# A hybrid S5 / RG-LRU / GLA block on one core: decay logarithms in a new layout, value weights by single blocks, decays behind the chain, and a new order at the turn to the up projection

## The chip, the core and the metric

The kernel runs on one core of a Trainium2 chip. The metric is the time of one execution on the device in microseconds (us), the median of several runs. A core has a matrix engine (TensorE, PE in the profile), a vector engine (VectorE, DVE), a scalar engine (ScalarE, ACT), GpSimd (POOL), and SyncE (SP), which here only issues DMA transfers. Each engine works through its own instructions in order and waits on semaphores for the others. PE's results go to PSUM, from where DVE or ACT fetch them.

## The reference

One layer of a backbone over 1024 latent tokens, with 256 context tokens ahead of them, 1024 channels, in float32. All inputs are given to the kernel.

```python
u  = rms_norm(x) * (1 + scale) + shift        # and the same for the context
zl = split(u @ w_in);  zc = split(uc @ w_in)  # 5408 columns: S5, LRU x2, q, k, v, g, z, gates
s5  = S5 scan both ways over zl[0], then a gated linear unit
lru = RG-LRU both ways over a short convolution of zl[1], times gelu(zl[2])
gla = chunked gated linear attention, 4 heads, both ways, over q, k, v with the decay
      log_a = log_sigmoid(z[:, 16 d : 16 d + 16] @ w2[d] + b2[d]) / 16
y  = (g0 * (s5 @ w0) + g1 * (lru @ w1) + g2 * (gla @ w2)) @ w_out
h  = x + gate * y
u  = rms_norm(h) * (1 + scale) + shift
h  = h + gate * ((silu(conv3(u @ up)[gate half]) * conv3(u @ up)[value half]) @ down)
out = rms_norm(h)
```

The recurrent mixers scan the context first and start the latent scan from its final state. The 32 columns z, sixteen for each direction, give 512 decay logarithms for each token: four blocks of 128 rows, two per direction.

## The kernel before

Every matrix product is done in three passes of rounded halves: weights and activations are split into a high part (line 214, a cast on ACT) and a rest (line 215, a subtraction on POOL or DVE), called wh and wl for weights, uh and ul for the normed latent tokens, uch and ucl for the context. The output of a product of 512 tokens lies in a PSUM tile "ma" or "mb", of 256 context tokens in one of them; smaller things lie in four tiles "sm".

PE's instructions stand in the order in which the program is written (pe_order, line 444). The projections are a generator, proj_stream, whose parts the mixers interleave with their own products: at each point F(name) a mixer draws as many microseconds of projection work as the table FILL says. A second generator, background, makes the decay logarithms; one piece of it, a matmul on line 653 and its followers, comes after every BG-th step of the value projection. The projections stop at markers ("lru", "pc", "kv", "g") until the mixer allows them on. For the other engines the scheduler decides what stands where, except in a stretch at the start (start_order) and one at the turn to the up projection (norm_order, lines 1770 to 1891, and turn_order behind it), where the program's order holds.

The work before and around the change, in order of time:

- The LRU's scans, up to about 249 us: ACT and DVE work on blocks of 128 channels and 1280 tokens (lines 953 to 990), beside q, k and context projections on PE.
- z_steps makes z. It loads wz, splits it into one of three wh buffers (lines 687 and 688), and multiplies (lines 691 to 702). z for the context lies in lsw[3], for the latents in lsw[2], all in partitions 0 to 63.
- decay_logs makes one piece of the logarithms: a matmul (line 653), Abs, Relu and Exp on ACT (658, 660, 661), then a polynomial in which ACT squares into a buffer "tmp" (665) and DVE multiplies it on (666), three times; POOL subtracts and a DMA takes the result away. There are three buffers "tmp", and the result r lies in one of them from line 660 until the DMA has read it. Eight pieces of 512 latent tokens come first, then four of 256 context tokens.
- v_steps makes the value projection of ten blocks of 128 tokens. For each half of the value columns it takes two weights at once (take(2)), each a wh and a wl, and goes over groups of four blocks with both; its results go out by line 733.
- S5, from about 339 us: its prepared state (lines 1148 to 1174), then the first of its products (1166, 1187, 1215), DVE's sums (1219 to 1222) and scans.
- GLA, from about 520 us: for each head, decays() makes the running sums (scans on lines 1287 and 1288, then 1291 to 1300) and states() runs an 18-step chain of the state (line 1362) and copies it out (1365, 1366). The next head's decays() stands in the program behind the present head's states and its first scores. Beside it PE makes projections (528 to 532), which ACT fetches (795, 606).
- The turn, 880 to 980 us: the output projection (284 to 286) leaves h, whose squares are added up (1729, 1730), summed over channels on PE (279) and spread again (273). The up projection's products are combinations of four token quarters (Strassen's and Winograd's way): product operands T1 to T4 and B11 to B22, weight combinations (1629), and results in PSUM banks bka to bkd (lines 839 to 841), read by lines 1641 to 1672. p1, p3 and p4 are such products; z57 copies C (1666), adds D (1667) and z (1668). Four subtractions of one h block from another stand on POOL (1752).

Of the kernel before, what the change touches and what calls it, by code (L numbers as in the profile page):

```python
# [82 lines left out]
BG = 4  # L83
# [26 lines left out]
def tile_kernel(tc, I, out, dbg=None):  # L110
# [567 lines left out]
    zw = []  # L678

    def z_steps():  # L680
# [7 lines left out]
        V.tensor_tensor(zz[:, :, 32:64], wz3, f32(zz[:, :, 0:32]), OP.subtract)  # L688
        p = one()
# [4 lines left out]
        zc = lsw[3][0:64, 0:256]  # L694
        S.copy(zc, p[0:64, 0:256])
# [12 lines left out]
        zw.append((zs + [zc], w2))  # L708

    def v_steps(blocks):  # L710
        for hv in range(2):
            ws = take(2)
            for b0 in range(0, len(blocks), 4):
                bs = blocks[b0:b0 + 4]
                p = two()
                for i, b, k in [(i, b, 4 * kh + k) for kh in range(2) for i, b in enumerate(bs) for k in range(4)]:
                        o = p[i // 2][:, i % 2 * 256:(i % 2 + 1) * 256]
                        h, l = ws[k // 4]
                        sl = slice((k % 4) * 256, (k % 4 + 1) * 256)
                        if b < 2:  # L720
                            ah, al = uch[:, k, b * 128:(b + 1) * 128], ucl[:, k, b * 128:(b + 1) * 128]
                        else:
                            j, bb = divmod(b - 2, 4)
                            ah, al = uh[j][:, k, bb * 128:(bb + 1) * 128], ul[j][:, k, bb * 128:(bb + 1) * 128]
                        last = k == KT - 1 and i % 2 == 1
                        PE.matmul(o, ah, h[:, sl], start=(k == 0 and i % 2 == 0), stop=False, skip_group_check=True)
# [4 lines left out]
                for i0 in range(0, len(bs), 2):  # L731
                    t = pt()
                    S.copy(t, p[i0 // 2])
                    S.dma_start(vsp[bs[i0] * 128:(bs[i0] + 2) * 128, hv * 256:(hv + 1) * 256]
                                .rearrange("(a t) v -> t a v", a=2), t.rearrange("p (a v) -> p a v", a=2))
# [7 lines left out]
    def proj_stream():  # L743
# [13 lines left out]
        yield from marker("lru")  # L757
        for b in range(2):
# [519 lines left out]
    class Head:  # L1278
# [59 lines left out]
        def states(self):  # L1338
# [22 lines left out]
            for step in range(1, 19):  # L1361
                V.scalar_tensor_tensor(Sd[:, step], Sd[:, step - 1], self.dec[:, step:step + 1], Sd[:, step],
                                       OP.mult, OP.add)
# [115 lines left out]
    for h in range(4):  # L1479
# [6 lines left out]
        head.scores(0)  # L1486
        if nxt:
            nxt.decays()
# [120 lines left out]
    class Pair:  # L1609
# [53 lines left out]

        def z57(self):
            w, z = self.gv[1][:, tl[0]], self.gv[1][:, tl[1]]
            S.copy(w, self.C)
# [44 lines left out]
    for j in range(2):  # L1711
        sl = tl[j]
        acc = pt()
        for m in range(8):
# [16 lines left out]
            if j == 1 and m == 3:  # L1731
                for i in range(2):
# [41 lines left out]
    for m in (6, 7):  # L1774
        SY.dma_start(hsp[m][:, tl[1]], hT[m][:, tl[1]])
    q[1].sums((5,))
# [4 lines left out]
    q[1].p1()  # L1781
    rq = rstd_cols(st, 4, small[:, 12:16])
    q[1].sums((6, 7))
# [3 lines left out]
    bcast(pr, rq, 4)  # L1787
    for i in range(2):
        product(q[i].A, q[i].w[2], B21, False)
# [85 lines left out]
    q[0].load(3, 4)  # L1875
    nxt.open("b")
# [12 lines left out]
    q[1].z6()  # L1889
    q[1].z57()  # L1890
# [8 lines left out]
    for i in range(2, HID):  # L1899
# [12 lines left out]
        product(pair.D, pair.w[7], T3, True)  # L1912
        pair.z57()
# [395 lines left out]
```

## Time and profile before

| | us |
|---|---|
| median of 3 runs (lowest, highest) | 1599.78 (1599.44, 1605.92) |
| the profiled execution | 1601.49 |
| its span | 1599.7 |
| PE busy in the span | 1521.8 (95%) |
| DVE busy | 1092.8 (68%) |
| ACT busy | 770.1 (48%) |
| POOL busy | 461.3 (29%) |

The profiled execution lasted 1.79 us more than its span, and 1.71 us more than the median. PE's idle time is what bounds the kernel from below: 78 us. The granted clock of PE has two levels, 1.2 and 2.4 GHz; a mean of 0.66 in a stretch of 5 us says that about two thirds of it were at the lower level.

### The profile page before, as it was taken

How to read it: one execution, taken by the hardware profiler on the slowest of the kernel's cores; microseconds unless marked ns; L12 is line 12 of the kernel's file. 1: busy time of each engine (PE TensorE's matmuls, PEld its weight loads, DVE VectorE, ACT ScalarE, POOL GpSimd, SP SyncE). 2: the span in 40 equal slices, each digit the busy share in tenths (PEclk: the TensorE clock that was granted, in tenths of full speed). 3: DMA queues.
4: the chain of work that ended last, by engine and by line, in shares of the span. 5: the costliest groups of instructions: out<-in, count | busy, mean ns of one | idle time of the engine just before them, and what ended most of it. 6: DMA issues, size and time to landing. Idle time of an engine off the chain costs nothing. (4 is left out here: it accounts for less than half of the span.)

```text
span 1599.7 us, 21566 instructions
## 1 busy us (share of the span) xinstructions
PE 1521.8 (95%) x8144; PEld 1254.7 (78%) x8144; DVE 1092.8 (68%) x1620; ACT 770.1 (48%) x1221; POOL 461.3 (29%) x291
## 2 busy tenths in 40 slices
PE   5999999799998999999999988999999999999997
PEld 4888867677886788788888767788888888878887
DVE  4533469879876624533461689888888888899962
ACT  4423766665543643443233455444444444444661
POOL 3313333431122323222236534333333333000032
PEclk9999999899999999999999999999999999999999
DMA  9763633221224244231474321222222222974203
GB/s 346 242 224 93 208 109 110 93 90 58 64 61 144 70 139 130 77 86 60 144 246 159 130 88 40 92 80 79 80 91 81 80 80 100 370 248 157 93 27 106
DMA packets 93785, 198.91 MB, mean 124 GB/s; under 512 B 13489, under 2 KB 34865, under 8 KB 93553
## 3 DMA queue, kind: packets, MB, share of 16 engines
q1 hardware_dynamic: 81968, 181.62, 33.9%
q10 hardware_dynamic: 11712, 15.91, 2.9%
q8 instruction: 64, 1.05, 0.3%
q14 instruction: 41, 0.33, 0.1%
HBM read 158.98 MB, written 38.52 MB: 123 GB/s over the span
## 5 line engine op out<-in xcount | busy, mean ns | idle before, releaser
L215 POOL TENSOR_TENSOR wl<-wr,wh 128x1024 fp32r<-128x1024 f32 (+2 forms) x87 | 183.4, 2109 | 455.7 <-ACT wh L214 428.5
L214 ACT CAST wh<-wr 128x1024 fp32r<-128x1024 f32 (+2 forms) x87 | 77.3, 891 | 139.6 <-issue 41.9
L215 POOL TENSOR_TENSOR wp<-tmp,wp 128x512 fp32r<-128x512 f32 x44 | 74.1, 1701 | 220.4 <-ACT wp L214 203.4
L528 PE MATMUL ma<-uh,wh 128*128 128x512 f32 x272 | 118.0, 434 | 4.5 <-ACT pt L795 4.5
L528 PE MATMUL mb<-uh,wh 128*128 128x512 f32 x272 | 107.2, 394 | 0.0
L530 PE MATMUL ma<-ul,wh 128*128 128x512 f32 x272 | 107.0, 393 | 0.0
L530 PE MATMUL mb<-ul,wh 128*128 128x512 f32 x272 | 106.9, 393 | 0.0
L532 PE MATMUL mb<-uh,wl 128*128 128x512 f32 x272 | 106.7, 392 | 0.0
L532 PE MATMUL ma<-uh,wl 128*128 128x512 f32 x272 | 106.4, 391 | 0.0
L214 ACT CAST wp<-tmp 128x512 fp32r<-128x512 f32 x78 | 46.5, 619 | 93.0 <-DVE tmp L1629 92.9
L1693 DVE SCALAR_TENSOR_TENSOR ca<-gv,vec,ca 128x1023 f32<-128x1023 f32 (+2 forms) x66 | 61.4, 954 | 23.7 <-ACT ca L1685 23.6
L214 ACT CAST wp<-hd 128x512 fp32r<-128x512 f32 x88 | 52.8, 618 | 49.1 <-PE bkd L1998 25.9
L214 ACT CAST wp<-wr 128x512 fp32r<-128x512 f32 x97 | 58.2, 620 | 36.4 <-DMA wr<-in_wdn_dram 17.4
L1696 DVE SCALAR_TENSOR_TENSOR ca<-gv,vec,ca 128x1023 f32<-128x1023 f32 (+2 forms) x66 | 70.6, 1093 | 0.1
L528 PEld LDWEIGHTS ma<-uh,wh 128*128 128x128 f32 x272 | 51.8, 190 | 20.7 <-issue 6.5
L2178 POOL TENSOR_TENSOR acc<-acc,tmp 128x256 f32<-128x256 f32 (+1 forms) x9 | 9.0, 1002 | 182.8 <-ACT tmp L2175 182.7
L215 DVE TENSOR_TENSOR wp<-hd,wp 128x512 fp32r<-128x512 f32 x88 | 60.7, 708 | 1.3 <-ACT wp L214 1.1
L530 PEld LDWEIGHTS ma<-ul,wh 128*128 128x128 f32 x272 | 51.6, 190 | 11.5
L532 PEld LDWEIGHTS ma<-uh,wl 128*128 128x128 f32 x272 | 51.4, 189 | 11.5
L532 PEld LDWEIGHTS mb<-uh,wl 128*128 128x128 f32 x272 | 51.3, 189 | 11.4
L530 PEld LDWEIGHTS mb<-ul,wh 128*128 128x128 f32 x272 | 51.3, 189 | 11.3
L528 PEld LDWEIGHTS mb<-uh,wh 128*128 128x128 f32 x272 | 52.0, 191 | 9.5 <-issue 1.4
(628 smaller groups left out, 4661.9 us busy)
## 6 DMA issues: line engine op xcount, KB each, us to landing
wa<-in_ada_dram SPq DMA_DIRECT2D x96, 256.0 KB
wr<-in_wup_dram SPq DMA_DIRECT2D x46, 512.0 KB
wr<-in_win_dram SPq DMA_DIRECT2D x40, 512.0 KB
wr<-in_wdn_dram SPq DMA_DIRECT2D x22, 512.0 KB
hd<-hid SPq DMA_DIRECT2D x22, 512.0 KB
hid<-ca SPq DMA_DIRECT2D x21, 512.0 KB
wr<-in_wout_dram SPq DMA_DIRECT2D x16, 512.0 KB
tmp<-in_wdn_dram SPq DMA_DIRECT2D x22, 256.0 KB
```

The source lines that it names most:

```text
L214: S.copy(h, src)
L215: lo.tensor_tensor(l, src, f32(h), OP.subtract)
L528: PE.matmul(p[j], h[:, kk], uh[j][:, k], start=f, stop=False)
L530: PE.matmul(p[j], h[:, kk], ul[j][:, k], start=False, stop=False)
L532: PE.matmul(p[j], l[:, kk], uh[j][:, k], start=False, stop=e)
L1693: V.scalar_tensor_tensor(a[:, t0_ + 1:t0_ + 1 + n1], x[:, o:o + n1], fw[0], a[:, t0_ + 1:t0_ + 1 + n1], OP.mult, OP.add)
L1696: V.scalar_tensor_tensor(a[:, t0_ + c - 1:t0_ + n - 1], x[:, o + c:o + n], fw[2], a[:, t0_ + c - 1:t0_ + n - 1], OP.mult, OP.add)
L2178: G.tensor_tensor(acc, acc, sq, OP.add)
```

## The change

Six edits. First, the z weights are split in a function of their own, z_prep, called at the marker "lru", into a buffer tmp instead of a wh; w2 is loaded twice, into partitions 0 to 63 and 64 to 127, and the two latent halves of z lie in these partition halves. Second, r lies in lsw[3] (two halves in turn) and no longer in a tmp; the context's z lies in a tmp. The four context pieces come first, and a piece comes after every sixth step instead of every fourth. Third, v_steps takes one weight at a time and goes over all blocks with it, with up to four PSUM tiles. Fourth, the next head's decays are issued after the last step of the present head's chain. Fifth, the four subtractions of h blocks go from POOL to DVE. Sixth, in the turn the products p1 and B21 stand elsewhere, and the copy of C is a step of its own, c57, ahead of the next product.

```diff
-BG = 4
+BG = 6
...
-            r = tmp()[:, :n]
+            r = lsw[3][:, par * 512:par * 512 + n]
...
-        zs, w2 = zw[0]
+        zs, zc, w2 = zw[0]
+        yield from decay_logs(0, 256, zc, w2[0])
         for j in range(2):
-            yield from decay_logs(C + j * 512, 512, zs[j], w2)
-        yield from decay_logs(0, 256, zs[2], w2)
+            yield from decay_logs(C + j * 512, 512, zs[j], w2[j])
...
+    def z_prep():
         wz = wraw(I["wz"], 256)
-        zh, _ = whl()
-        zz = zh[:, 0:512].rearrange("p (k m) -> p k m", k=KT)
-        w2 = lsw[3][0:64, 256:768]
-        SY.dma_start(w2, I["w2"])
+        zz = tmp([128, 512], F32R).rearrange("p (k m) -> p k m", k=KT)
+        w2 = [lsw[2][64 * j:64 * j + 64, 512:1024] for j in range(2)]
+        for w in w2:
+            SY.dma_start(w, I["w2"])
...
+    def z_steps():
+        zz, w2 = zp[0]
...
-        zc = lsw[3][0:64, 0:256]
-        S.copy(zc, p[0:64, 0:256])
+        zct = tmp([64, 256])
+        S.copy(zct, p[0:64, 0:256])
...
-            z = lsw[2][0:64, j * 512:(j + 1) * 512]
+            z = lsw[2][64 * j:64 * j + 64, 0:512]
...
         for hv in range(2):
-            ws = take(2)
-            for b0 in range(0, len(blocks), 4):
-                bs = blocks[b0:b0 + 4]
-                p = two()
-                for i, b, k in [(i, b, 4 * kh + k) for kh in range(2) for i, b in enumerate(bs) for k in range(4)]:
...
+            p = [one("ab"[i % 2]) for i in range(len(blocks) // 2)]
+            for kh in range(2):
+                (h, l), = take()
+                for i, b in enumerate(blocks):
+                    o = p[i // 2][:, i % 2 * 256:(i % 2 + 1) * 256]
+                    for k in range(4):
...
         yield from marker("lru")
+        z_prep()
...
-                V.scalar_tensor_tensor(Sd[:, step], Sd[:, step - 1], self.dec[:, step:step + 1], Sd[:, step],
+                self.last = V.scalar_tensor_tensor(Sd[:, step], Sd[:, step - 1], self.dec[:, step:step + 1],
...
         if nxt:
-            nxt.decays()
+            with tc.issue_after(head.last.ins):
+                nxt.decays()
...
+        def c57(self):
+            S.copy(self.gv[1][:, tl[0]], self.C)
+
         def z57(self):
             w, z = self.gv[1][:, tl[0]], self.gv[1][:, tl[1]]
-            S.copy(w, self.C)
...
             if j == 1 and m == 3:
+                for k in range(4, KT):
+                    x = hT[k][:, tl[0]]
+                    V.tensor_tensor(x, x, hT[k - 4][:, tl[0]], OP.subtract)
...
-                    if k > 3:
-                        x = hT[k][:, tl[0]]
-                        G.tensor_tensor(x, x, hT[k - 4][:, tl[0]], OP.subtract)
...
+    q[1].p1()
     q[1].sums((5,))
...
     sums(st, accs[1], 4, by=per_d)
-    q[1].p1()
     rq = rstd_cols(st, 4, small[:, 12:16])
+    product(q[0].A, q[0].w[2], B21, False)
...
     bcast(pr, rq, 4)
+    product(q[1].A, q[1].w[2], B21, False)
     for i in range(2):
-        product(q[i].A, q[i].w[2], B21, False)
         q[i].open("bcd" if i == 0 else "cd")
...
     q[0].load(3, 4)
+    q[0].c57()
     nxt.open("b")
...
     q[1].z6()
+    q[1].c57()
     q[1].z57()
```

The same c57 stands ahead of z57 in the steady loop, where it moves nothing.

PE where S5's products begin, before (528 to 532 are projections into ma and mb, 1166 and 1187 are S5's; the last piece of the decay logarithms stands 169 rows further up):

```order
L532 MATMUL mb_3171<-uh_110,wl_2883 128x512
L1166 MATMUL sm_3232<-con,s_3221 128x128 x2
L528 MATMUL ma_3170<-uh_109,wh_2882 128x512
L528 MATMUL mb_3171<-uh_110,wh_2882 128x512
L530 MATMUL ma_3170<-ul_111,wh_2882 128x512
L530 MATMUL mb_3171<-ul_112,wh_2882 128x512
L532 MATMUL ma_3170<-uh_109,wl_2883 128x512
L532 MATMUL mb_3171<-uh_110,wl_2883 128x512
L1166 MATMUL sm_3256<-con,s_3245 128x128 x2
L528 MATMUL ma_3285<-uh_109,wh_3160 128x512
```

The same place after, where line 1166 has become 1174:

```order
L532 MATMUL mb_3124<-uh_110,wl_2808 128x512
L1174 MATMUL sm_3202<-con,s_3191 128x128 x2
L528 MATMUL ma_3123<-uh_109,wh_2807 128x512
L528 MATMUL mb_3124<-uh_110,wh_2807 128x512
L530 MATMUL ma_3123<-ul_111,wh_2807 128x512
L530 MATMUL mb_3124<-ul_112,wh_2807 128x512
L532 MATMUL ma_3123<-uh_109,wl_2808 128x512
L532 MATMUL mb_3124<-uh_110,wl_2808 128x512
L653 MATMUL sm_3226<-lsw_1457 128x512
L1174 MATMUL sm_3243<-con,s_3215 128x128 x2
L528 MATMUL ma_3272<-uh_109,wh_2943 128x512
```

The last piece, now one of 512 tokens, stands between the two S5 products.

ACT in the GLA at the start of the next head's decays, before (1295 to 1300 belong to decays, 795 fetches a projection, 1365 and 1366 copy the state chain's result):

```order
L1360 COPY gl_5878<-sm_5908 64x2x128
L1295 ACTIVATE gl_6000<-gl_5997 64x20
L1296 ACTIVATE gl_6000<-gl_5997 64x4
L1297 ACTIVATE gl_6000<-gl_5997 64x16
L1418 DMA yosp<-gl_5662 128x1024
L1300 ACTIVATE gl_6004<-gl_6004 128x1280
L795 ACTIVATE pt_6013<-ma_5857 128x512
L795 ACTIVATE pt_6014<-mb_5858 128x512
L214 CAST wh_6019<-wr_6017 128x256
L1365 COPY gl_5877<-gl_5878 64x1024
```

After, where 1295 to 1300 have become 1303 to 1308, 795 is 803, and 1365 and 1366 are 1373 and 1374:

```order
L1373 COPY gl_5864<-gl_5865 64x1024
L1374 COPY gl_5864<-gl_5865 64x1024
L1426 DMA yosp<-gl_5649 128x1024
L803 ACTIVATE pt_6000<-ma_5844 128x512
L803 ACTIVATE pt_6001<-mb_5845 128x512
L1374 COPY gl_5864<-gl_5865 64x1024
L1373 COPY gl_5864<-gl_5865 64x1024
L214 CAST wh_6006<-wr_6004 128x256
L214 CAST wh_6030<-wr_6028 128x1024
L1303 ACTIVATE gl_5987<-gl_5984 64x20
L1304 ACTIVATE gl_5987<-gl_5984 64x4
L1305 ACTIVATE gl_5987<-gl_5984 64x16
L1415 DMA acc_6221<-gsp 128x512
L1308 ACTIVATE gl_5991<-gl_5991 128x1280
```

The fetches and the chain's copies stand ahead of the decays now.

POOL at the turn, before (1752 are the subtractions of h blocks, 215 the rests of weights):

```order
L215 TENSOR_TENSOR wl_7637<-wr_7634,wh_7636 128x1024
L266 TENSOR_TENSOR tmp_7631<-tmp_7631,small 128x4
L215 TENSOR_TENSOR wl_7714<-wr_7711,wh_7713 128x1024
L1752 TENSOR_TENSOR h_7294<-h_7294,h_7286 128x512
L1752 TENSOR_TENSOR h_7296<-h_7296,h_7288 128x512
L1752 TENSOR_TENSOR h_7298<-h_7298,h_7290 128x512
L1752 TENSOR_TENSOR h_7300<-h_7300,h_7292 128x512
L215 TENSOR_TENSOR wl_7750<-wr_7747,wh_7749 128x1024
L215 TENSOR_TENSOR wl_7790<-wr_7787,wh_7789 128x1024
L215 TENSOR_TENSOR wl_7826<-wr_7823,wh_7825 128x1024
```

POOL at the same place after:

```order
L215 TENSOR_TENSOR wl_7624<-wr_7621,wh_7623 128x1024
L266 TENSOR_TENSOR tmp_7618<-tmp_7618,small 128x4
L215 TENSOR_TENSOR wl_7697<-wr_7694,wh_7696 128x1024
L215 TENSOR_TENSOR wl_7733<-wr_7730,wh_7732 128x1024
L215 TENSOR_TENSOR wl_7777<-wr_7774,wh_7776 128x1024
L215 TENSOR_TENSOR wl_7813<-wr_7810,wh_7812 128x1024
L215 TENSOR_TENSOR wp_7852<-wr_7772,wp_7852 128x512
```

DVE after, where the subtractions now stand as line 1746 (215 the rest of an activation, 1742 the sum of squares, 1734 the residual):

```order
L1746 TENSOR_TENSOR h_7281<-h_7281,h_7273 128x512
L215 TENSOR_TENSOR B21l<-h_7287,B21h 128x512
L1742 TENSOR_TENSOR pt_7576<-pt_7576,sq_7727 128x512
L1734 SCALAR_TENSOR_TENSOR h_7279<-sm_7736,md,h_7279 128x512
L1746 TENSOR_TENSOR h_7283<-h_7283,h_7275 128x512
L1746 TENSOR_TENSOR h_7285<-h_7285,h_7277 128x512
L1742 TENSOR_TENSOR pt_7576<-pt_7576,sq_7763 128x512
L1746 TENSOR_TENSOR h_7287<-h_7287,h_7279 128x512
```

POOL goes from one weight's rest to the next; DVE has four more instructions between the residuals of the output projection.

## Rows read from the trace of the kernel before

**Rows 1.** Waits of PE by line and releaser: total us, times, longest us.

```profile
PE ma L726 <- ACT wh L214: 7.6, 1, 7.6
...
PE ma L528 <- ACT pt L795: 4.5, 2, 3.8
PE ma L691 <- DVE wh L688: 3.9, 1, 3.9
PE sm L653 <- ACT tmp L660: 3.7, 2, 2.8
...
PE sm L286 <- POOL wl L215: 2.5, 1, 2.5
PE ma L727 <- POOL wl L215: 2.4, 1, 2.4
...
PE bkb L279 <- DVE pt L1730: 1.6, 1, 1.6
...
PE sm L1393 <- ACT gl L1366: 1.0, 1, 1.0
```

**Rows 2.** Windows: from:to, length, busy PE, PEld, DVE, ACT, POOL, PEclk, DMA, GB/s.

```profile
210.00:215.00 5.00, 5.00 (x21) 3.08 (x19) 2.38 (x2) 4.97 (x8) 0.12 (x1) 0.66 0.45 157
248.60:270.00 21.40, 21.40 (x131) 17.08 (x132) 19.51 (x66) 14.06 (x22) 7.82 (x4) 1.00 0.52 165
270.00:290.00 20.00, 17.18 (x114) 15.29 (x114) 19.81 (x49) 16.18 (x25) 4.87 (x4) 0.91 0.18 66
290.00:310.00 20.00, 9.01 (x52) 7.84 (x51) 17.89 (x33) 10.80 (x19) 10.23 (x6) 0.74 0.30 103
310.00:330.00 20.00, 20.00 (x147) 18.94 (x148) 15.13 (x30) 12.83 (x25) 10.71 (x5) 1.00 0.23 79
330.00:353.00 23.00, 21.00 (x103) 16.75 (x101) 14.75 (x25) 19.19 (x32) 6.24 (x4) 1.00 0.31 104
```

**Rows 3.** Timeline of DVE in the LRU: start us, us, what it does.

```profile
175.71 2.82 DVE L975 TENSOR_TENSOR_SCAN lt<-la,lt 128x1280 f32<-128x1280 f32 x1
...
215.63 4.88 DVE L975 TENSOR_TENSOR_SCAN lt<-la,lt 128x1280 f32<-128x1280 f32 x1
```

**Rows 4.** Timeline of DVE in S5's preparation, then of PE at S5's second products.

```profile
337.50 2.19 DVE L1148 TENSOR_TENSOR s<-s 128x640 f32<-128x640 f32 x1 [2.18 <-ACT s L1153]
...
353.03 0.49 PE L1187 MATMUL sm<-s,s 128*16 128x128 f32 x3 [2.03 <-DVE s L1221]
```

**Rows 5.** Timeline of ACT at a change of the function table among the decays.

```profile
279.79 0.62 ACT L661 ACTIVATE lsw<-lsw 128x512 f32<-128x512 f32 x1
280.43 1.28 ACT L1074 ACT_TABLE_LOAD   x1
281.73 0.45 ACT L1074 ACTIVATE s<-s 128x288 f32<-128x288 f32 x1
```

**Rows 6.** Timeline of DVE and ACT at a head's decays in the GLA.

```profile
660.36 2.57 DVE L1299 TENSOR_TENSOR gl<-gl,gl 128x1280 f32<-128x1280 f32 x1
...
662.97 1.27 ACT L1300 ACTIVATE gl<-gl 128x1280 f32<-128x1280 f32 x1 [4.79 <-DVE gl L1299]
664.26 0.60 ACT L795 ACTIVATE pt<-ma 128x512 f32<-128x512 f32 x1
```

**Rows 7.** Timeline of POOL and DVE at the turn.

```profile
905.85 1.29 POOL L1752 TENSOR_TENSOR h<-h,h 128x512 f32<-128x512 f32 x1 [0.63 <-DVE B21l L215]
...
916.43 0.75 DVE L1722 SCALAR_TENSOR_TENSOR h<-sm,md,h 128x512 f32<-128x512 f32 x1 [3.66 <-PE sm L286]
...
924.58 1.79 DVE L1629 TENSOR_TENSOR tmp<-wr,wr 128x512 f32<-128x512 f32 x1
```

**Rows 8.** Timeline of PE at product p3 and of DVE's addition of D (line 1667).

```profile
974.65 0.50 PE L839 MATMUL bkc<-B22h,wp 128*128 128x512 f32 x1 [4.61 <-ACT gv L1666]
...
975.19 0.67 DVE L1667 TENSOR_TENSOR gv<-gv,bkd 128x512 f32<-128x512 f32 x1
```

More of the change, by code (lines that the diff above doesn't have):

```diff
@@ L671, in background @@
     def background():
-        zs, w2 = zw[0]
+        zs, zc, w2 = zw[0]
+        yield from decay_logs(0, 256, zc, w2[0])
         for j in range(2):
-            yield from decay_logs(C + j * 512, 512, zs[j], w2)
-        yield from decay_logs(0, 256, zs[2], w2)
+            yield from decay_logs(C + j * 512, 512, zs[j], w2[j])
         reached.add("ls")
-    zw = []
-    def z_steps():
+    zw, zp = [], []
+    def z_prep():
         wz = wraw(I["wz"], 256)
-        zh, _ = whl()
-        zz = zh[:, 0:512].rearrange("p (k m) -> p k m", k=KT)
-        w2 = lsw[3][0:64, 256:768]
-        SY.dma_start(w2, I["w2"])
+        zz = tmp([128, 512], F32R).rearrange("p (k m) -> p k m", k=KT)
+        w2 = [lsw[2][64 * j:64 * j + 64, 512:1024] for j in range(2)]
+        for w in w2:
+            SY.dma_start(w, I["w2"])
         wz3 = wz.rearrange("p (k m) -> p k m", k=KT)
@@ L688, in z_steps @@
         V.tensor_tensor(zz[:, :, 32:64], wz3, f32(zz[:, :, 0:32]), OP.subtract)
+        zp.append((zz, w2))
+    def z_steps():
+        zz, w2 = zp[0]
         p = one()
@@ L704, in z_steps @@
         for j in range(2):
-            z = lsw[2][0:64, j * 512:(j + 1) * 512]
+            z = lsw[2][64 * j:64 * j + 64, 0:512]
             S.copy(z, p[j][0:64])
             zs.append(z)
-        zw.append((zs + [zc], w2))
+        zw.append((zs, zct, w2))
     def v_steps(blocks):
         for hv in range(2):
-            ws = take(2)
-            for b0 in range(0, len(blocks), 4):
-                bs = blocks[b0:b0 + 4]
-                p = two()
-                for i, b, k in [(i, b, 4 * kh + k) for kh in range(2) for i, b in enumerate(bs) for k in range(4)]:
-                        o = p[i // 2][:, i % 2 * 256:(i % 2 + 1) * 256]
-                        h, l = ws[k // 4]
-                        sl = slice((k % 4) * 256, (k % 4 + 1) * 256)
+            p = [one("ab"[i % 2]) for i in range(len(blocks) // 2)]
[4 more added lines that the diff above has]
+                    for k in range(4):
+                        sl = slice(k * 256, (k + 1) * 256)
+                        ka = 4 * kh + k
                         if b < 2:
-                            ah, al = uch[:, k, b * 128:(b + 1) * 128], ucl[:, k, b * 128:(b + 1) * 128]
+                            ah, al = uch[:, ka, b * 128:(b + 1) * 128], ucl[:, ka, b * 128:(b + 1) * 128]
                         else:
                             j, bb = divmod(b - 2, 4)
-                            ah, al = uh[j][:, k, bb * 128:(bb + 1) * 128], ul[j][:, k, bb * 128:(bb + 1) * 128]
-                        last = k == KT - 1 and i % 2 == 1
-                        PE.matmul(o, ah, h[:, sl], start=(k == 0 and i % 2 == 0), stop=False, skip_group_check=True)
+                            ah, al = uh[j][:, ka, bb * 128:(bb + 1) * 128], ul[j][:, ka, bb * 128:(bb + 1) * 128]
+                        last = ka == KT - 1 and i % 2 == 1
+                        PE.matmul(o, ah, h[:, sl], start=(ka == 0 and i % 2 == 0), stop=False, skip_group_check=True)
                         PE.matmul(o, ah, l[:, sl], start=False, stop=False, skip_group_check=True)
@@ L730, in v_steps @@
                             yield 3 * COL
[L731 to L735, printed above, removed]
+                    if kh and i % 2:
+                        t = pt()
+                        S.copy(t, p[i // 2])
+                        S.dma_start(vsp[(b - 1) * 128:(b + 1) * 128, hv * 256:(hv + 1) * 256]
+                                    .rearrange("(a t) v -> t a v", a=2), t.rearrange("p (a v) -> p a v", a=2))
     def marker(name):
@@ L1361, in states @@
             for step in range(1, 19):
-                V.scalar_tensor_tensor(Sd[:, step], Sd[:, step - 1], self.dec[:, step:step + 1], Sd[:, step],
-                                       OP.mult, OP.add)
+                self.last = V.scalar_tensor_tensor(Sd[:, step], Sd[:, step - 1], self.dec[:, step:step + 1],
+                                                   Sd[:, step], OP.mult, OP.add)
             for c0 in (0, 8):
@@ L1912, in tile_kernel @@
         product(pair.D, pair.w[7], T3, True)
+        pair.c57()
         pair.z57()
```

## The prediction

> **What bounds the kernel now.** I read the page's busy shares first: PE is busy 95% of the span, so the kernel can win only what PE waits, and what the waits cost in clock. Then the waits of PE by line [rows 1]. Eight lines bear on this change: weights for values (7.6 and 2.4 us), a projection tile that ACT fetches late in the GLA (4.5 in two, 3.8 of it at one place), the z weights (3.9), decay logarithms (3.7 in two), a weight's rest in the output projection (2.5), the squares' sum (1.6) and a state copy (1.0); a ninth wait is that for the copy of C before p3 (4.61 [rows 8]). Third, the windows, which show two things [rows 2]. After the wait for the z weights PE's granted clock is 0.66 over 5 us, part of them at 1.2 instead of 2.4 GHz: 0.34 x 5 = 1.7 us lost behind the wait. And from 248.6 us, where DVE ends the LRU, to S5 at 353, DVE is the engine without room: busy 19.51 + 19.81 + 17.89 + 15.13 + 14.75 = 87.1 of 104.4 us, 17.3 idle, while PE does 9.0 us of work in the 20 from 290 to 310. At the end of that stretch PE waits for DVE too (2.03) [rows 4].
>
> **The front: z weights, layout, single blocks.** Moving the z weights ahead of two q and two k projections takes away 3.9. The logarithms' r leaves the three buffers that the squares turn in, so the two waits of 3.7 go. With one weight per turn each weight is in use for 96 matmuls, and the next is split meanwhile: 7.6 + 2.4 = 10.0 go. Together 17.6. At three of these restarts (z, first logarithms, values) the clock falls; the 1.7 measured at one, taken for each, makes 5.1. Sum 22.7: PE alone would be at S5's second products at 353.0 - 2.0 - 22.7 = 328.3.
>
> DVE can't follow. The same instructions stand ahead of S5's sums as before (194 then, 193 now), so 87.1 us stay. Two things can shrink. The start: an LRU scan takes 4.88 us where POOL works beside it and 2.82 where it doesn't [rows 3], and POOL's splits move; I take 245 for the LRU's end (2.06 for the scan, and some for its neighbours), with 248.6 and 243 as ends. The idle: of 17.3, S5's own preparation must wait for ACT (2.18 at one place [rows 4]), and three more of its kind I can't remove; I take 6, with 3 and 10 as ends. So 245 + 87.1 + 6 = 338.1, plus 0.6 to PE's start as now: 338.7 against 353.0, a gain of 14.3. Behind it, S5's next products wait for DVE once more, and part of the lead goes there; those waits are not shorter for an earlier start, but the clock falls as now at a new long wait. I take 1.7 off: **12.6**. Ends: 248.6 + 87.1 + 10 = 345.7 gives 5; 243 + 87.1 + 3 = 333.1 gives 18.
>
> So I expect the waits of [rows 1] to go and a new one of about 10 us (338.7 - 328.3) to appear at S5's first products, or at a logarithm matmul right before.
>
> The layout changes the order of the pieces too. The last one is now of 512 tokens and stands between S5's products; ACT switches its function table twice more. A switch costs ACT 1.30 us here: the activation ahead ends at 280.41, the next starts at 281.73 [rows 5], so 2.6 for two, on an engine with 3.8 us idle in the last window [rows 2]: inside the ends above. The Trainium skill speaks against this edit with more: "ScalarE: Activation LUTs", section "What ACT_TABLE_LOAD costs", has 1.28 us for the load and 1.38 for a drain ahead of it, 2.66 a switch. By that the two would cost 5.3 and the forecast would be later by at most 2.7. The rows have the load and no room for the drain, so I go by them.
>
> **Decays behind the chain.** ACT's fetch of the tile that PE wants stands behind an Exp of 1.27, which waited 4.79 for a product of 2.57 that DVE put among the chain's steps [rows 6]. Now the fetches are ahead of both. That takes 3.8, 1.7 of clock (from the other restart) and, since the chain isn't interrupted by scans, the 1.0 for its copy: **6.5**. The scans come some 7 us later; their readers are next head's products, beside which PE has projections. If that cover were gone it would cost up to 3.5, so 3 to 6.5.
>
> **The turn.** Four subtractions leave POOL, where the last ends at 907.14 and the rest of a weight that PE waits for starts after it [rows 7]: 2.5 go, and 1.7 of clock: 4.2. On DVE they cost 0.67 each, a plain addition of that shape [rows 8], or 1.79, one beside POOL's work [rows 7]: 2.7 or 7.2. What hides them is DVE's idle before the next residual, 3.66 [rows 7]; at 7.2 PE would wait 3.5 for a residual's tile. I take 2.7, hidden, since the tiles of the output projection are four. The Trainium skill warns of just this: "GPSIMD Engine Reference", section "Specifications", has SBUF interfaces of GpSimd shared with VectorE, and contention with VectorE instructions that read two inputs from SBUF, as these do. It gives no time; by it the turn's sum would be that with 7.2.
>
> The product ahead of the squares' sum hides its 1.6, but the spread behind it now comes after more matmuls (12 of 512 columns, at 2.4 GHz an estimate of 0.21 us each, 2.6 in all, of which about 2 no longer lie behind the sum), and DVE waits for it: -0.5, with +1 and -2 as ends. The copy of C: PE no longer waits 4.6 for it at p3, but p4 right behind writes the bank that holds D, which DVE reads until 975.86 [rows 8]. p3 would start at 974.65 - 4.61 = 970.0 and end 2.6 later, so 3.2 of wait moves to p4. The gain is 4.6 - 3.2 = 1.4, less a little for DVE's order: 1.3, from 0 to 2.5. Together **5.0**, from 1 to 7.7.
>
> Sum 12.6 + 6.5 + 5.0 = 24.1 on the profiled execution's span of 1599.7: 1575.6, and with 1.8 around it 1577.4. That execution lies 1.7 above the median, which I forecast: 1599.8 - 24.1 = **1575.7**, so 1576. Ends of the parts: 5 + 3 + 1 = 9 and 18 + 6.5 + 7.7 = 32.
>
> **The rivals.** *PE decides in front.* If DVE's work between the LRU and S5 shrinks, because contention with POOL or waits for ACT were most of it, PE gains all 22.7 + 2.0. With 11.5 from the rest that is 36: 1564. For it: DVE has 17.3 idle. Against: 87.1 of busy time stand in the way and PE's 328.3 would leave 248.6 to 328.3 = 79.7 for them. Chance 0.1.
>
> *The front gives nothing.* DVE keeps its pace with all its idle time, since this comes from the back and forth with ACT over each piece, and the PE waits of [rows 1] merely gather at S5. Then 11.5 remain: 1588. For it: DVE's share is 99% at 270 to 290. Against: it falls to 64 to 76% from 310, where the pieces come at PE's pace, and PE is earlier there. Chance 0.2.
>
> *The last pieces hold S5.* In the new order the last logarithms and S5's preparation share the tmp buffers, ACT and DVE at one place. If they run in turn instead of side by side, the stretch from 290 costs the sum of both engines: 28.7 + 28.0 + 33.9 = 90.6 instead of 63, and S5 starts at 353 - 3.6 + 27.6 = 377, 24 late. With 11.5 from the rest that is 1612. It makes the kernel slower from the point where S5's second products come later than 353 + 11.5 = 364.5, which asks for 15 of these 27.6. Against: the instructions are those of before, and in the window with the most of both (330 to 353) they overlap by 11 us. Chance 0.04.
>
> *The copies move and no more.* p4 and the new wait at the squares take back the whole turn, and the GLA's decays come late for the next head: 12.6 + 3 + 1, 1583. Chance 0.11.
>
> **How the numbers follow.** The forecast has 0.55, the four rivals 0.1, 0.2, 0.04 and 0.11. The range reaches from the first rival to just beyond the second: 1564 to 1590. A difference of 0.5%, 8 us, is about what a measurement of this kernel can tell from no change. Faster by more than that is all under 1591.8: forecast, first, second and last rival, less what lies beyond their ends (of the second, a quarter): 0.90. Same 0.06, slower 0.04.
>
> **What would show it.** In the profile of after the waits at 691, 726, 727 (now 733, 734), 653, the 3.8 at 528 and the 2.5 at 286 should be gone. At S5's first products (1166, 1187, now 1174, 1195) or at the last logarithms a wait of some 10 us for DVE should stand, with S5's second products at about 338. DVE should be busy over 90% from 250 to 338. At the turn p4 (line 839 into bkd) should wait some 3 us in place of p3. If S5's second products start before 330, or after 350, the front's step is wrong; if PE waits at the residuals of the output projection, the subtractions aren't hidden.

## The result

The changed kernel takes 1585.64 us, median of four runs (1585.10 to 1586.42); the kernel before, with one more run beside it, 1602.55 (1599.44 to 1605.92). The ratio is 0.9894, 95% interval 0.9868 to 0.9921: about 17 us faster, where 24 were forecast. The profiled execution took 1585.10 with a span of 1583.3, 16.4 less than the span of 1599.7 before. The page of after reads PE 1514.1 us busy (96%), DVE 1091.0, ACT 772.4, POOL 461.5.

Where the 16.4 us came from can be read at four products whose start stands in both traces (PE's timeline, us from the start of the span):

| start of | before | after | gained so far | gained in the part | forecast for it |
|---|---|---|---|---|---|
| S5's second products (1187, now 1195) | 353.03 | 349.47 | 3.6 | | 14.3 |
| S5's last products (1240, now 1248) | 486.44 | 479.58 | 6.9 | 6.9 | 12.6 |
| GLA's last products (1393, now 1401) | 750.95 | 738.88 | 12.1 | 5.2 | 6.5 |
| the up projection's first (839, now 847) | 927.11 | 910.65 | 16.5 | 4.4 | 4.2 |
| the end | 1599.7 | 1583.3 | 16.4 | -0.1 | 0.8 |

PE's waits of after, by line and releaser (total, times, longest):

```profile
PE mb L528 <- ACT pt L740: 5.4, 1, 5.4
PE ma L528 <- ACT pt L740: 5.2, 1, 5.2
PE ma L705 <- ACT pt L740: 4.9, 1, 4.9
PE bkd L847 <- DVE gv L1679: 4.7, 3, 3.2
```

The waits of [rows 1] on lines 726, 727, 691, 653, 286, 279 (for the squares) and 1393 are gone, and 528 waits only 0.7 us for line 803 (795 before). But three waits of together 15.5 us, all in front of S5, have one new releaser: line 740 (733 before), where ACT fetches a tile of the value projection. The wait of 10 us that I expected at S5's first products for DVE isn't there. The windows of after that answer to [rows 2] (busy PE, PEld, DVE, ACT, POOL, then the granted clock):

```profile
270.00:290.00 20.00, 19.74 (x145) 17.41 (x144) 18.74 (x40) 14.46 (x23) 7.81 (x5) 1.00 0.30 88
290.00:310.00 20.00, 18.78 (x132) 16.04 (x132) 14.70 (x31) 7.47 (x14) 15.25 (x3) 1.00 0.19 63
310.00:330.00 20.00, 10.59 (x33) 7.43 (x34) 13.87 (x18) 18.46 (x27) 8.94 (x5) 0.74 0.29 102
```

DVE, which I had made the bound, is idle for 5.3 us from 290 to 310, and POOL shows 15.25 us for three instructions. The timeline there, first POOL, then SP, ACT and DVE:

```profile
286.33 1.46 POOL L667 TENSOR_TENSOR lsw<-lsw,lsw 128x512 f32<-128x512 f32 x1 [1.41 <-DVE lsw L666]
292.71 11.69 POOL L667 TENSOR_TENSOR lsw<-lsw,lsw 128x512 f32<-128x512 f32 x1 [4.92 <-DVE lsw L666]
...
304.42 0.32 SPq L668 DMA_DIRECT2D lsp<-lsw  x1
...
307.23 0.69 ACT L660 ACTIVATE lsw<-sm,small 128x512 f32<-128x512 f32 x1 [8.26 <-DMA lsp<-lsw]
...
313.40 0.57 ACT L740 COPY pt<-ma 128x512 f32<-128x512 f32 x1
...
302.42 0.42 DVE L1170 TENSOR_TENSOR s<-s,s 128x256 f32<-128x256 f32 x1
302.75 0.49 DVE L1157 TENSOR_SCALAR s<-s 128x640 f32<-128x640 f32 x1
308.54 0.69 DVE L662 SCALAR_TENSOR_TENSOR lsw<-lsw 128x512 f32<-128x512 f32 x1 [5.30 <-ACT lsw L661]
```

Read it from the top. The subtraction that ends a piece of the logarithms takes POOL 1.46 us at one place and 11.69 at the next. The long one begins at 292.71 and ends at 304.40, 1.16 us after DVE's unbroken run ends at 303.24: 22 instructions since 292.55, 18 of them with two inputs in SBUF, each started before the one ahead had ended. So POOL's time reads as an ordinary subtraction behind a wait for DVE. Only then goes out the transfer that frees that half of lsw[3]; ACT, which must write r there (660), has waited 8.26 us for it; and behind this instruction stand, on ACT, the fetches (740) that PE waits for.

My reading, which the experiments test, is that the front lost its gain to a chain of four queues: DVE keeps POOL out, POOL's subtraction holds the transfer, the transfer holds ACT, ACT holds PE's tiles.

### The profile page after: what moved, and what is told of

Same layout as the page of the kernel before. It is cut to its first block, busy times and chain, and to the rows that moved or that the text cites. A ratio compares the mean times of both kernels' runs of the same rounds, so it can differ in the third digit from the quotient of the medians.

```text
span 1583.3 us, 21584 instructions
## 1 busy us (share of the span) xinstructions
PE 1514.1 (96%) x8144; PEld 1247.4 (79%) x8144; DVE 1091.0 (69%) x1624; ACT 772.4 (49%) x1223; POOL 461.5 (29%) x287
## 5 line engine op out<-in xcount | busy, mean ns | idle before, releaser
L1370 DVE SCALAR_TENSOR_TENSOR gl<-gl,gl 128x128 f32<-128x128 f32 x72 | 31.2, 433 | 52.4 <-ACT gl L1368 38.1
L528 PEld LDWEIGHTS mb<-uh,wh 128*128 128x128 f32 x272 | 51.5, 190 | 15.5 <-ACT pt L740 5.9
```

Of the source, the lines that this page charges most:

```text
L528: PE.matmul(p[j], h[:, kk], uh[j][:, k], start=f, stop=False)
L1370: self.last = V.scalar_tensor_tensor(Sd[:, step], Sd[:, step - 1], self.dec[:, step:step + 1], Sd[:, step], OP.mult, OP.add)
```

## The experiments

Three theories on the front. **P**: the chain just told. **D**, the prediction's: DVE's own work sets S5's start, and the rest is a by-product. **A**: the order of work on ACT is enough. All experiments change the changed kernel, not the one before. Nearly all are single runs. The four runs of the changed kernel lie within 1.3 us; a product's start in a trace is good to about 2 us: the three kernels below whose front is that of the changed kernel (the decays at once, the subtractions on POOL, the turn's order) start S5's last products at 479.51, 481.41 and 479.55, against 479.58.

**The subtraction on DVE.**

```diff
-            G.tensor_tensor(r, r, acc, OP.subtract)
+            V.tensor_tensor(r, r, acc, OP.subtract)
```

> The changed kernel with the subtraction that ends each piece of the decay logarithms (line 667) on VectorE instead of GpSimd. In the changed kernel one of these took 11.7 us on GpSimd, ScalarE then waited 8.3 us for the half of lsw[3], and TensorE waited 5.2 and 5.4 us for tiles that ScalarE had not fetched. Theory P (VectorE's unbroken run of two-input instructions keeps GpSimd's subtraction out, and everything behind it is late): ScalarE's wait falls under 2 us, TensorE's two waits mostly go, S5's second products start at 340 to 345 instead of 349.5, and the time is 1575 to 1580 against 1585. Rival D (VectorE's own work sets S5's start): VectorE gets 8 x 0.68 + 4 x 0.42 = 7.1 us more, S5's second products start 4 to 7 us later, and the time is 1588 to 1592.

Measured: 1586.08, S5's second products at 350.82. As P had it for the subtraction the result is a miss, and D's 4 to 7 us didn't come either. The trace says why (POOL, SP, ACT):

```profile
289.12 25.14 POOL L215 TENSOR_TENSOR wl<-wr,wh 128x1024 fp32r<-128x1024 f32 x2 [3.79 <-ACT wh L214]
...
311.78 0.33 SPq L205 DMA_DIRECT2D wr<-in_win_dram  x1
312.20 0.38 SPq L668 DMA_DIRECT2D lsp<-lsw  x1
...
316.24 0.69 ACT L660 ACTIVATE lsw<-sm,small 128x512 f32<-128x512 f32 x1 [8.31 <-DMA lsp<-lsw]
```

Now a weight's rest is kept out: two that take 2.4 us each when alone (as at 304.35 in the changed kernel) take 25.14, nearly all of it the first. The load of the next weight waits for that buffer at the head of SP's queue, the logarithms' transfer stands behind the load, and ACT waits 8.31 us for it as before. The chain has another first link and the same end.

**Relu last, and a small step.**

```diff
-            S.activation(r, p[:, :n], AF.Relu, bias=nb2[:, h:h + 1], scale=-1.0)
...
+            S.activation(r, p[:, :n], AF.Relu, bias=nb2[:, h:h + 1], scale=-1.0)
             G.tensor_tensor(r, r, acc, OP.subtract)
```

> The changed kernel with Relu, the instruction that writes r, behind the three squares instead of ahead of Exp. Theory P: the subtraction on GpSimd may still be long, but ScalarE meets the full half of lsw[3] four instructions later, so that VectorE gets work meanwhile; the waits of TensorE for tiles fall from 10.6 us to 3 to 7, time 1577 to 1583. Rival D: nothing changes, 1585 within 1.5.

```diff
-            V.scalar_tensor_tensor(acc, e, LOGQ_R, e, OP.add, OP.mult)
+            for c in (slice(0, 32), slice(32, n)):
+                V.scalar_tensor_tensor(acc[:, c], e[:, c], LOGQ_R, e[:, c], OP.add, OP.mult)
```

> The changed kernel with VectorE's first step of each piece's polynomial (line 662) split into one of 32 columns and one of the rest: 12 more VectorE instructions of 0.1 to 0.2 us. In the traces GpSimd started its work beside small VectorE instructions (32 columns, which then took 1.0 to 2.4 us instead of 0.17), and not in the run where all had 256 columns or more. Theory P with that addition: GpSimd gets in at the small step, the subtraction stays under 4 us, ScalarE's wait falls under 3, time 1576 to 1582. Rival D, or P without the addition: the long subtraction stays, 1585 to 1588.

Both 1584.77, second products at 349.37 and 348.64: no change. The long subtraction stayed in both, with 12.99 us in the first; here in the one with the small step:

```profile
292.11 11.74 POOL L668 TENSOR_TENSOR lsw<-lsw,lsw 128x512 f32<-128x512 f32 x1 [4.98 <-DVE lsw L667]
```

The addition to P, that POOL gets in at an instruction of 32 columns, is wrong; such a step at 295.67 didn't let it in.

**The fetches on DVE.**

```diff
-                        S.copy(t, p[i // 2])
+                        V.tensor_copy(t, p[i // 2])
```

> The changed kernel with the value projection's results fetched by VectorE instead of ScalarE (line 740): 12 fetches of some 0.6 us more for VectorE, as many fewer for ScalarE. Rival A (the order on ScalarE, where the fetches stand behind whatever waits, costs the time): TensorE's waits for these tiles (4.9, 5.2 and 5.4 us) go, S5's second products start by 344, time 1576 to 1581. Theory P: the waits at these tiles shrink, but ScalarE still waits 8 us for the half of lsw[3], and TensorE waits at the logarithm matmuls or at S5 instead; S5's second products within 3 us of 349.5, time 1582 to 1588.

1586.23, second products at 349.03: A falls. The three waits became four of 3.7, 1.7, 4.1 and 3.4 us, for DVE and ACT. The time is P's, but P's wait isn't: ACT has no wait for the logarithms' transfer here, and POOL's longest subtraction takes 5.60 us. With 12 fetches more on DVE, this run tells against A and nothing for P.

**Four halves in turn.** Relu comes last and writes into e, which is dead by then; e goes round four halves.

```diff
-            e = lsw[0][:, par * 512:par * 512 + n]
+            e = lsw[lsn[0] // 2 % 2 * 3][:, par * 512:par * 512 + n]
...
+            r = e
```

> The changed kernel with Relu behind the squares, written into the buffer of e, which is dead by then; e takes turns among four halves (lsw[0] and lsw[3]) instead of two. Nothing is left out. Theory P (VectorE's unbroken run keeps GpSimd out, and ScalarE is held by r's half, which is freed only by the transfer behind GpSimd's subtraction): with four in turn ScalarE's 8.3 us wait for the transfer goes, TensorE's waits for tiles behind the values (5.2 and 5.4) fall to under 5 in all, S5's second products start at 341 to 346, time 1576 to 1581. GpSimd's long subtraction may stay, then VectorE itself waits for it at the next piece but one, by 1 to 3 us. Rival D (VectorE sets the start of S5): second products within 2 us of 349.5, time 1583 to 1587.

1581.46, second products at 347.08, S5's last at 476.01: half of what P hoped, more than D allows. POOL's subtraction is long again, and now DVE itself stops for it, in two rows:

```profile
293.25 12.03 POOL L667 TENSOR_TENSOR lsw<-lsw,lsw 128x512 f32<-128x512 f32 x1 [4.65 <-ACT lsw L658]
...
305.31 2.84 DVE L660 SCALAR_TENSOR_TENSOR lsw<-lsw 128x512 f32<-128x512 f32 x1 [1.20 <-POOL lsw L667]
```

DVE ended its run at 304.12, and 1.16 us later POOL was done. ACT had no long wait for the transfer, and PE's two waits fell from 5.2 and 5.4 to 4.5 and 2.5. Why not further, this run doesn't show.

**No POOL among the logarithms.** The subtraction on DVE, and the rests of the weights too from z to the last piece.

```diff
-            wq.append(wblock(src, src.shape[-1]))
+            wq.append(wblock(src, src.shape[-1], V if zw and "ls" not in reached else G))
...
-            G.tensor_tensor(r, r, acc, OP.subtract)
+            V.tensor_tensor(r, r, acc, OP.subtract)
```

> The changed kernel with GpSimd relieved of its work among the decay logarithms: the subtraction (line 667) and the rests of the weights taken from the z products to the last piece are on VectorE, 12 subtractions of 0.4 to 0.7 us and some 6 rests of 1.2: 14 us more VectorE work. Theory P: nothing is left to be kept out, ScalarE's wait of 8 us for a transfer and TensorE's waits for tiles (10.6 us) go, S5's second products start at 342 to 350 in spite of the added work, time 1577 to 1586. Rival D (VectorE's work sets the start of S5): second products at 357 to 363, time 1592 to 1599.

1571.33: 14 us under the changed kernel, the fastest of all, in a single run, and more than P had forecast. S5's second products start at 335.95, 13.5 earlier, although DVE has 12 subtractions and 6 rests more ahead of them, 13.6 us by themselves. The windows from the LRU's end to S5's second products, of the changed kernel and of this one:

```profile
247.25:349.47 102.22, 91.33 (x550) 75.47 (x548) 84.24 (x201) 72.54 (x119) 43.07 (x21) 0.95 0.31 100
246.42:335.95 89.53, 89.53 (x554) 74.95 (x552) 83.80 (x222) 70.72 (x115) 6.42 (x3) 1.00 0.35 116
```

DVE is busy 83.8 us instead of 84.2 in spite of the added work, since without POOL beside it other instructions take less (a multiplication on line 666 takes 2.83 us beside POOL at 311.83 in the changed kernel, 0.68 alone). Its idle time falls from 18.0 to 5.7 us. In three windows of 20 us:

```profile
270.00:290.00 20.00, 20.00 (x148) 17.85 (x147) 18.43 (x44) 16.30 (x26) 4.02 (x2) 1.00 0.38 126
290.00:310.00 20.00, 20.00 (x140) 17.40 (x139) 20.00 (x39) 15.42 (x23) 0.00 (x0) 1.00 0.27 93
310.00:330.00 20.00, 20.00 (x89) 14.55 (x88) 17.95 (x32) 18.47 (x32) 0.00 (x0) 1.00 0.24 79
```

PE has no gap and the full clock. Of its three waits in front of S5 one is left, at 214.81:

```profile
PE ma L705 <- ACT pt L740: 5.0, 1, 5.0
```

This settles P against D: more work on DVE, and S5 starts earlier. The subtraction alone, moved to DVE, gained nothing as long as the rests stayed on POOL; with neither left there, nothing waits for an engine that DVE keeps out.

**The z weights late.**

```diff
         yield from marker("lru")
-        z_prep()
...
         zz, w2 = zp[0]
```

(with z_prep() called ahead of the last line)

> The changed kernel with z_prep called at the start of z_steps instead of at the marker, so that the z weights are split late as before (into a tmp as in the changed kernel). Theory Z (ScalarE is full from 205 to 215 us, so that removing the wait for the z weights only brought TensorE to a wait for a tile that ScalarE fetches at 213.7): the 4.9 at that tile turns back into a wait of 3 to 4 at the z weights, S5 and the end move by less than 1.5 us, time 1584 to 1587. Rival of the prediction (3.9 and 1.7 of clock were gained): everything behind is 3 to 5.6 us later, time 1588 to 1591.

1582.23. The wait is back:

```profile
210.35 0.30 PE L698 MATMUL ma<-uch,tmp 128*64 128x256 f32 x1 [3.79 <-DVE tmp L690]
```

But the latents' first z product starts at 214.66 against 214.32: there the early weights gained 0.3 us. In the changed kernel it waits 4.94 for a tile that ACT fetches at 213.70, behind two weight casts and a table load; ACT is full there. Behind that wait its z products at first take 0.63 us each, where with the late weights they take 0.39, and the last z product starts at 228.24 against 227.00: the early weights have lost 1.2 us by then. S5's last products come 3.3 us earlier with the late weights. POOL's long instructions lie elsewhere in this run (11.96 us for two and 5.87 for one); that the other 2 us come from that is not shown.

**The values as before.**

```diff
-            p = [one("ab"[i % 2]) for i in range(len(blocks) // 2)]
-            for kh in range(2):
-                (h, l), = take()
...
+            ws = take(2)
+            for b0 in range(0, len(blocks), 4):
+                bs = blocks[b0:b0 + 4]
+                p = two()
```

> The changed kernel with v_steps as before: two weights at once, groups of four blocks. Theory of the prediction: TensorE waits 7 to 10 us for the second pair of value weights again, S5's second products start 4 to 8 us later, time 1589 to 1594. Rival (what holds ScalarE and GpSimd sets S5's start, and the wait for weights only stands in for the wait for tiles): within 2 us of 1585, with the waits for tiles of the values (5.2, 5.4) gone.

1585.89, S5's second products at 345.77 and its last at 478.10, against 349.47 and 479.58. The rival holds: single blocks gained nothing. The waits of 7.6 and 2.4 for the weights didn't come back, so another part of the change had removed them, by elimination the layout. The waits of 5.2 and 5.4 for tiles are gone; three of 2.3, 1.7 and 2.0 stand in their place. POOL is kept out twice (10.09 us for two subtractions, 9.23 for one), and ACT waits 7.2 and 5.1 us for the transfers.

**Both faster edits.**

> The changed kernel with both edits that were faster in one look: four halves in turn for e and r with Relu last (S5's last products 3.6 us earlier than in the changed kernel), and the z weights split late (3.3 us earlier). Theory P: both shorten the same wait, ScalarE's and GpSimd's delay in front of S5, so that they don't add up: time 1577 to 1582, at best 2 below the better one. Rival (they are separate, one at 210 us and one at 300): 1575 to 1578, 7 us under the changed kernel's 1585.

1580.50, median of four runs (1579.53 to 1581.21), beside 1603.30 for the kernel before: ratio 0.9857, interval 0.9841 to 0.9874. That is 5.1 under the changed kernel, beyond the spread of either. But the two don't add up: S5's last products at 474.49, 1.5 earlier than with the four halves alone. That agrees with P.

**The decays at once.**

```diff
-            with tc.issue_after(head.last.ins):
-                nxt.decays()
+            nxt.decays()
```

> The changed kernel with the next head's decays issued where the program has them, not behind the chain. By the trace the edit won 1.2 us at the first head and 5.1 at the third, less 0.7 later. Theory: these 5 to 6 come back, the wait of TensorE for ScalarE's fetch of a projection tile (line 803) is 3.5 to 4 us again, time 1590 to 1592. Rival (they were won by the shift of all engines, not by the order): less than 2 come back, 1585 to 1587.

1590.44, 4.8 more. From the first to the last GLA product it takes 195.3 us instead of 189.9, 5.5 more, and the wait is there:

```profile
PE ma L528 <- ACT pt L803: 4.5, 2, 3.8
```

**The subtractions on POOL.**

```diff
-                    V.tensor_tensor(x, x, hT[k - 4][:, tl[0]], OP.subtract)
...
+                        G.tensor_tensor(x, x, hT[k - 4][:, tl[0]], OP.subtract)
```

> The changed kernel with the four subtractions of h blocks on GpSimd, behind the splits, as before. Theory: TensorE waits 2 to 3 us for a weight's rest in the output projection again and loses 1.5 to 2 in clock, time 1588 to 1590. Rival (the turn's later chain on VectorE takes the place of that wait, because the four instructions now lie on it): within 1.5 of 1585.

1591.96. The second half of the output projection takes 44.34 us instead of 39.98 (before: 44.36), and the wait is back. Some 2 us of the 6.3 that this run is slower stand ahead of S5, where the edit changes nothing.

```profile
PE sm L286 <- POOL wl L215: 2.5, 1, 2.5
```

**The turn's order as before.**

```diff
-    q[1].p1()
     q[1].sums((5,))
...
     sums(st, accs[1], 4, by=per_d)
+    q[1].p1()
     rq = rstd_cols(st, 4, small[:, 12:16])
-    product(q[0].A, q[0].w[2], B21, False)
...
     for i in range(2):
+        product(q[i].A, q[i].w[2], B21, False)
...
-    q[0].c57()
...
+    q[0].c57()
     q[0].z57()
     q[0].p3()
```

> The changed kernel with the turn's order as before (p1 behind the squares' sum, both B21 products together, the copy of C at its old place), and with the four subtractions still on VectorE. Theory: what the new order takes from the waits at the sum (1.6) and at p3 (4.6) it gives back at the spread and at p4 (3.15 in the changed kernel), so the stretch from the up projection's first product to the end stays within 1 us of the changed kernel's 672.7, time 1584 to 1587. Rival of the prediction (0.8 gained, up to 3.5): the stretch is 0.8 to 3.5 longer, time 1586 to 1589.

1588.44. From the up projection's first product to the end it takes 677.5 us instead of 672.7, 4.9 more: above both expectations. PE's timeline at the squares' sum and at p3, then the windows of this kernel around the sum:

```profile
914.04 1.60 PE L279 MATMUL bkb<-over_d,pt 128*128 128x1 f32 x8 [2.03 <-DVE pt L1742]
...
960.19 0.80 PE L847 MATMUL bkc<-B22h,wp 128*128 128x512 f32 x1 [4.58 <-ACT gv L1675]
```

```profile
909.00:914.00 5.00, 3.01 (x14) 2.11 (x12) 4.24 (x8) 3.29 (x6) 0.00 (x0) 1.00 0.81 281
914.00:921.00 7.00, 6.96 (x22) 5.80 (x23) 3.24 (x6) 0.00 (x0) 1.40 (x1) 0.53 0.45 164
```

Counted from the up projection's first product, the sum's input comes 0.5 us later than in the kernel before; PE waits 2.03 instead of 1.56 us, and its clock falls: 0.53 granted over the next 7 us, 3.3 us lost, where in the kernel before it stayed at 1.00 behind the wait:

```profile
931.50:936.00 4.50, 4.40 (x26) 3.90 (x27) 3.21 (x7) 0.39 (x1) 1.38 (x1) 1.00 0.29 88
```

The spread follows 6.7 us behind the sum instead of 3.8. So most of the 4.9 is clock, and the clock is no fixed price of a wait. p4's wait of 3.15 us is the same in the changed kernel and in the one with the decays at once, but behind it the granted clock is 1.00 in the first and 0.72 in the second:

```profile
960.43 0.47 PE L847 MATMUL bkd<-T4h,wp 128*128 128x512 f32 x1 [3.15 <-DVE gv L1679]
965.39 0.52 PE L847 MATMUL bkd<-T4h,wp 128*128 128x512 f32 x1 [3.15 <-DVE gv L1678]
```

```profile
960.43:966.43 6.00, 6.00 (x26) 4.93 (x27) 5.88 (x6) 3.65 (x6) 6.00 (x5) 1.00 0.00 0
965.39:971.39 6.00, 6.00 (x19) 4.78 (x20) 5.88 (x6) 3.76 (x6) 6.00 (x5) 0.72 0.00 0
```

In the eleven other kernels with the new order the stretch to the end takes 672.8 to 674.8 us, so the old order's 677.5 is above them all; that it must cost the clock at the sum each time is not shown.

## Why the prediction was right, and where it wasn't

The range (1564 to 1590) held the time, the direction was right, and the middle was 9.6 us too low; of the gain 17 of 24 came. That the range held is in part luck: the front came out by another mechanism than I had told, and the range took it in because it reached as far as the rival in which the front gives nothing. My sign of a wrong front, S5's second products after 350, was missed by half a microsecond (349.47). DVE was busy 83% from 250 to 338 (73.4 of 88.0 us) where I had written over 90%, and the wait of 10 us for it wasn't there. The waits that were to go went, p4 waits 3.15, and no residual waits.

**The front** is the step that failed: 6.9 us for 12.6. Not in its sum of PE's waits, 22.7: the kernel without POOL among the logarithms, with one wait of 5.0 left and 1.6 us of clock lost behind it (0.31 of 5.2 us), starts S5's second products at 335.95, and 328.3 + 5.0 + 1.6 = 334.9. Wrong was a term of DVE's sum, 245 + 87.1 + 6: the idle time. The changed kernel has 247.3 + 84.2 + 18.0 = 349.5; of before's 17.3 us of idle none went, where I had all but 6 go. In the kernel without POOL the sum is 246.4 + 83.8 + 5.7 = 335.9, with an idle time like the one I forecast. So "DVE can't follow" is not what held S5 back. What DVE waits for is ACT, 5.3 us at one place, and the new waits of PE stand at value tiles, 10.6 of them; their cause is an instruction that I had not priced at all: POOL's subtraction, 1.3 to 3.1 us before for 512 tokens, 11.7 after. I had the price of that sharing in my rows, an LRU scan of 4.88 beside POOL and 2.82 alone [rows 3], and read it as DVE's loss only.

Why POOL is shut out for so long here, and wasn't before, stays open. A run of DVE without a break isn't enough: in the kernel before it has no break over 0.11 us from 252.8 to 290.9 (99% busy at 270 to 290 [rows 2]), and the five subtractions there take 1.3 to 1.8 us on POOL. The longest, 3.13 us, ended 1.1 us after DVE itself had stopped for it:

```profile
284.96 1.51 POOL L667 TENSOR_TENSOR tmp<-tmp,lsw 128x512 f32<-128x512 f32 x1 [4.46 <-DVE lsw L666]
...
300.64 3.13 POOL L667 TENSOR_TENSOR tmp<-tmp,lsw 128x512 f32<-128x512 f32 x1 [5.29 <-DVE lsw L666]
...
303.80 2.54 DVE L662 SCALAR_TENSOR_TENSOR lsw<-lsw 128x256 f32<-128x256 f32 x1 [1.16 <-POOL tmp L667]
```

Of the front's three parts, the layout is what gained, by elimination; no run takes it back alone. The early z weights gained 0.3 us at the first latent product (predicted 3.9 and 1.7 of clock) and cost 1.2 by the last, about 3 further on. Single blocks gained nothing (predicted 10.0). The z step took a wait that was the last to end for the only one: behind it a tile, in ACT's hands, was due at nearly the same time, and the clock fell behind that wait instead. The values' waits were gone without single blocks too.

**The second rival**, that the front gives nothing (1588), was the nearest of the other cases, by another way than I named. The slower rival, late pieces that hold S5, was not seen: in the changed kernel S5's second products were still 3.6 us early. The two more table loads were there (32 against 30). A switch took ACT 1.32 us again, from 311.35 to 312.67, so of the prediction's two prices the smaller held; what the two cost the kernel no run tells.

**Decays behind the chain**: mechanism right, 5.2 for 6.5. The trace has 1.1 by the second head, 5.1 at the third, and -1.0 behind it, where 0.7 and 0.5 us of new waits at lines 528 and 810 stand; that the decays, which now come beside them, are the reason is not shown. The experiment gives 5.5.

**The subtractions**: 4.4 for 4.2, with no wait at the residuals, and the experiment takes all of it back. But the price on DVE was wrong: I took 2.7 us for the four, and they take 6.5 (0.69, 2.24, 2.88 and 0.68), two of them beside rests on POOL:

```profile
890.14 0.69 DVE L1746 TENSOR_TENSOR h<-h,h 128x512 f32<-128x512 f32 x1
892.91 5.04 DVE L1746 TENSOR_TENSOR h<-h,h 128x512 f32<-128x512 f32 x2
898.48 0.68 DVE L1746 TENSOR_TENSOR h<-h,h 128x512 f32<-128x512 f32 x1
```

By the prediction's own 7.2 for four such, PE would have waited 3.5 us for a residual; it didn't. That they stayed hidden is luck by that reckoning.

**The order of the turn**: -0.1 for 0.8. p4 waits 3.15 us in place of p3's 4.61, as forecast with 3.2, and starts 2.2 us earlier counted from the first product of the up projection. Then PE waits 2.30 for a rest of weights, and its next product starts 97.5 us after the first, in the kernel before 97.7: weights set the pace there in both, and at the last product of the up projection the 2.2 are gone. Whether the two edits hang together is open. With the subtractions on POOL and the new order all of the 4.4 is gone; with them on DVE and the old order 4.1 stay and 4.9 are lost behind, of which 3.3 are clock.

Where the changed kernel missed the forecast of 1576, the fastest variant went past it: 1571.33, a single run, against 1585.64 and 1603.30.

## What to carry to other kernels

When a wait is taken away, look at what else was due at nearly the same time, and at what stands in the queues behind: here a busy DVE kept POOL out, and the bill came three queues later. Before calling an engine the bound by its busy time, ask what its idle time waits for, and how much of its busy time is another engine's doing: taking all of POOL's work in that stretch onto the "full" DVE gained 14 us, and left DVE no busier up to S5; taking a part of it gained nothing. And a single trace doesn't give the price of a wait in clock: at one place the same wait kept the clock in one kernel and lost it in another.

## What the runs showed of the hardware

A POOL instruction with SBUF inputs stood still beside DVE for 10 us and more: 11.69, 12.99, 11.74 and 12.03 us in four kernels for a subtraction of 128x512 that takes 1.28 at its best. Each ended 1.15 or 1.16 us after DVE's run did. Of the two rests that took 25.14, the first had ended by 311.78, when the load into its buffer went out, and DVE's first break stands at 309.54. The Trainium skill, page "SBUF — State Buffer", section "Who interferes with whom", calls the shared pair of ports an exclusive lock, and says that a DVE instruction with two SBUF inputs contends with a GpSimd instruction that reads SBUF. Of DVE's two-port modes the same section says that whoever issues first has the pair for the whole instruction, and the other is fully blocked. If two inputs block in the same way, a block would last one instruction, at most 1.35 us here (line 1156). The traces agree that POOL is blocked fully, and show it blocked through 22 of DVE's instructions. Elsewhere in the same stretch POOL did get in within half a microsecond (286.33, above), and so it did in the kernel before, beside a DVE without breaks. What decides that isn't shown; an instruction of 32 columns put into the run didn't help.

The second thing is the clock. Behind p4's wait of 3.15 us the granted clock was 1.00 over 6 us in the changed kernel and 0.72 in the one with the decays at once, with the same instructions around it. Behind the 2.03 us at the squares' sum it was 0.53 over 7 us, and the products there took 0.63 us instead of 0.39. What decides that isn't shown either.
